# The inverse roots of the norms: a power on GpSimd and one Newton step instead of an integer guess and three

## The chip, the cores and the metric

The kernel runs on one core of a Trainium2 chip. A core has a matrix engine (TensorE, PE in the profile, with its weight loads as PEld), a vector engine (VectorE, DVE), an activation engine (ScalarE, ACT), a general engine (GpSimd, POOL) and a queue that issues the transfers (SyncE, SP). Each engine works through its own list of instructions in order; semaphores let one wait for another. The metric is the device time of one execution in microseconds (us); lower is better.

## The reference, cut to what matters

One layer of a hybrid decoder over 1024 prompt tokens and 8 x 8 sample tokens, all in fp32, width 1024. Every sub-layer begins and ends with an RMS norm, and the state-space group has one of its own:

```python
def rmsnorm(x, g):
    y = x * lax.rsqrt(jnp.mean(x * x, axis=-1, keepdims=True) + EPS)
    return y * g

h = rmsnorm(x, g_mix_pre) * (1 + scale_m) + shift_m
proj = h @ w_in                        # short convolution group, z, x/B/C, dt
...                                    # convolutions, SSD scan in chunks of 128
yg = (y_ssd * silu(z)).reshape(b, L, 4, 256)
y_ssd = rmsnorm(yg, 1.0) * ssm_norm_g  # over 256 channels of each of 4 groups
mix = concatenate([y_sc, y_ssd]) @ w_out
x = x + gate_m * rmsnorm(mix, g_mix_post)
h2 = rmsnorm(x, g_ffn_pre) * (1 + scale_f) + shift_f
f = (silu(h2 @ w_gate) * (h2 @ w_up)) @ w_down
x = x + gate_f * rmsnorm(f, g_ffn_post)
```

So each token needs an inverse root of a mean square five times over: four times over 1024 channels, and once for each of four groups over 256.

## The kernel before, in words

The tokens are the 1024 of the prompt and the 64 samples, in 9 tiles of up to 128. Matrix products are exact to fp32 by splitting each factor into a high and a low part (ACT makes the high part, DVE the low one) and by three products for each pair of tiles (L334 to L336, L514 to L516, L1078 to L1080). Large products of the channel sub-layer and of the convolution group use a scheme with seven products for eight.

The stages, by time in the profile:

- 0 to 70 us, the head. Rows of x are loaded; ACT squares and sums them (`sum_sq`, L357), `rsqrt_of` gives the inverse roots (`rstd_x`), DVE scales the rows (`scale_x`, L372), PE turns them (`turn_x`, L383). This is done for three sets of three tiles, `norm_x(0)` before the rest, the others in a list of steps written out by hand (`steps`), which queues each step behind the one before on PE, DVE, ACT and POOL. Beside it come the modulation vectors from `w_ada` (`quarter_products` L244, `quarter_out` L251 to L258), the split of the first weights (on POOL for L312, behind the casts of `wdt`, L465 and L466) and the modulation (`modulate_in`, L479 to L481).
- to about 600 us, projections and the SSD scan, with the group norm (`norm`): squares on ACT, sums across channels by products with ones (L920), `rsqrt_of` for 9 columns at once, a product that spreads the roots over the partitions (`spread`, L291), and the scaling on DVE (L939). It is called four times.
- to about 1000 us, the output projection. Its tail (`mix_tail`) turns tiles back into rows (L1239), squares them and multiplies by the gate row (L1240, L1241, in `residual_rows`), takes `rsqrt_of`, adds to the residual on DVE (L1256), sums squares again (L357), takes `rsqrt_of` again, scales on ACT (L1348), and turns the rows back (L1356, L1358). It is run for tiles 0 to 3, 4 to 5 and 6 to 8, beside products of other tiles.
- to the end, the channel sub-layer, whose last products (`down`, L1758) run with `out_tail`, which again calls `residual_rows` for tiles 0 to 3, 4 to 6 and 7 to 8. For the first two of these the scaling is on ACT (L1253) and the addition on POOL (L1254); for the last set both are one DVE instruction (L1256), and the result is stored (L1716).

So `rsqrt_of` is called 16 times: three times for the head, four times in the group norm, six times in the tails of the output projection and three times at the end. It works on a small tile `sm` of 128 partitions and 2, 3, 4 or 9 columns, from a pool of four buffers that also holds the sums `ss`, which POOL clears (L1232).

The order of the instructions on each engine is settled when the kernel is built. A scheduler takes them in the order of the program, subject to the orders written by hand, and puts one ahead of another where it expects it to be ready sooner, by its own estimates. In the profile, instructions of other work therefore stand between those of one call of `rsqrt_of`.

Of the kernel before, what the change touches and what calls it, by code (L numbers as in the profile page):

```python
# [11 lines left out]
I32 = mybir.dt.int32  # L12
AF = mybir.ActivationFunctionType
ALU = mybir.AluOpType
PSUM = bass.MemoryType.PSUM

P = 128
# [16 lines left out]
def hymba_step(ctx, tc, i, o):  # L34
    nc = tc.nc
    mult, add, sub, mn, mx = ALU.mult, ALU.add, ALU.subtract, ALU.min, ALU.max
# [26 lines left out]
    def nm(s):  # L63
        ids[0] += 1
        return f"{s}_{ids[0]}"
# [23 lines left out]
    def const(shape, name, dt=F32):  # L89
        return cp.tile(shape, dt, tag=name, name=name)  # L90
# [104 lines left out]
    cT = const([P, KT, 32], "cT")  # L195
    nc.vector.tensor_copy(cT.rearrange("p a b -> p (a b)"), cps[:, :256])

    modT = const([P, 6, 2, 4, 9], "modT")
    modv = [modT[:, v].rearrange("p h q r -> p (h q) r") for v in range(6)]
    def ada_steps(rd):  # L200
# [74 lines left out]
    def rsqrt_of(src, w):  # L275
        n = src.shape[1]
        t = smp.tile([P, 3, 12], F32, tag="sm", name=nm("sm"))
        v, r, u = (t[:, j, :n] for j in range(3))
        nc.vector.tensor_scalar(v, src, 1.0 / w, EPS, op0=mult, op1=add)
        nc.vector.tensor_scalar(r.bitcast(I32), v.bitcast(I32), 1, None, op0=ALU.logical_shift_right)  # L280
        nc.vector.tensor_scalar(r.bitcast(I32), r.bitcast(I32), -1.0, float(0x5F3759DF), op0=mult, op1=add)
        for _ in range(3):
            nc.vector.tensor_tensor(u, r, r, op=mult)
            nc.vector.scalar_tensor_tensor(u, u, -0.5, v, op0=mult, op1=mult)
            nc.vector.scalar_tensor_tensor(r, u, 1.5, r, op0=add, op1=mult)
        return r

    def spread(r, n):
# [75 lines left out]
    def rstd_x(c):  # L364
        rx[c] = rsqrt_of(ssx[:, 3 * c:3 * c + 3], D)
# [199 lines left out]
    r = 0  # L565
# [97 lines left out]
    for b in range(3):  # L663
        aps = pz()
        n = 512 if b < 2 else NS
# [247 lines left out]
    def norm(g, y, new_sq, new):  # L913
# [9 lines left out]
        for c, (c0, n) in enumerate(CH):  # L923
# [7 lines left out]
            sums(c)  # L931
            yield
        r = rsqrt_of(ps[:, 0:9], 2 * P)
        yield
        for c, (c0, n) in enumerate(CH):
# [293 lines left out]
    def residual_rows(at, ts, G, res, u, banks, done, parts=((0, 4), (4, 4)), pool=(), halves=(slice(0, D),),  # L1229
                      squares=None):  # L1230
        ss = smp.tile([P, 3, 12], F32, tag="sm", name=nm("ss"))
        nc.gpsimd.memset(ss, 0.0)  # L1232
        for j, (k0, nk) in enumerate(parts):
            for tt, t in enumerate(ts):
                tn = size(t)
                cols = slice(k0 * P, (k0 + nk) * P)
                ps = banks[j][tt]()[:tn, :nk * P]
                for k in range(nk):
                    nc.tensor.transpose(ps[:, k * P:(k + 1) * P], at(k0 + k, t), ident)  # L1239
                nc.scalar.activation((squares or u[tt])[:tn, cols], ps, AF.Square, accum_out=ss[:tn, j, tt:tt + 1])  # L1240
                nc.vector.tensor_tensor(u[tt][:tn, cols], ps, (G[0] if t < 8 else G[1])[:tn, cols], op=mult)  # L1241
            if j < len(parts) - 1:
                yield
        n = len(ts)
        for j in range(1, len(parts)):
            nc.vector.tensor_tensor(ss[:, 0, :n], ss[:, 0, :n], ss[:, j, :n], op=add)
        r = rsqrt_of(ss[:, 0, :n], D)
        for tt, t in enumerate(ts):
            tn = size(t)
            for cols in halves:  # L1250
                v, w = res[tt][:tn, cols], u[tt][:tn, cols]
                if tt in pool:
                    nc.scalar.activation(w, w, AF.Copy, scale=r[:tn, tt:tt + 1])  # L1253
                    nc.gpsimd.tensor_tensor(v, v, w, op=add)  # L1254
                else:
                    nc.vector.scalar_tensor_tensor(v, w, r[:tn, tt:tt + 1], v, op0=mult, op1=add)  # L1256
                done(t, tn, res[tt], cols)
        yield
# [19 lines left out]
    for k in range(KT):  # L1278
        v = [(fx, btp, h2p)[(k > 3) + (k > 5)].tile([P, T], F32R, tag="bt" if k in (4, 5) else "fm", name=nm("hb"))
             for _ in range(2)]  # L1280
# [449 lines left out]
    for k in range(0, 6, 2):  # L1730
        raw = ffp[9, 0].tile([P, 2, D], F32, tag="ff", name=nm("rwd"))
        nc.sync.dma_start(raw, w_down[(16 + k) * P:(18 + k) * P, :].rearrange("(k p) n -> p k n", p=P))
        for kk in range(2):
            v = wdp.tile([P, 2, D], F32R, tag="wd", name=nm("wd"))
# [12 lines left out]
    for ts in ([0, 1, 2, 3], [4, 5, 6], [7, 8]):  # L1747
        c0, n = ts[0] * P, sum(map(size, ts))
# [47 lines left out]
```

## Time and profile before

| | |
|---|---|
| median of 3 runs | 1732.71 us (1731.55 to 1736.04) |
| the profiled execution, its time | 1732.75 us |
| its span | 1731.0 us |
| PE busy | 1682.0 us, 97% of the span |
| PE weight loads | 1600.0 us, 92% |
| DVE busy | 1147.9 us, 66%, 2194 instructions |
| ACT busy | 770.9 us, 45% |
| POOL busy | 185.7 us, 11%, 277 instructions |
| mean granted clock of PE | 0.99 |

The span is the time from the first to the last instruction of the profiled execution; the rest of its time lies around it. A row of a timeline gives the start in us, the duration in us, the engine, the line, the operation, the output and inputs, the shapes and how often; in brackets stands the idle time of the engine before it and what ended it. In a list by tile or by line, durations are in ns (least, median, most). In a table of windows each engine has its busy time in that stretch, then come the granted PE clock, the share of the transfer engines that was busy, and GB/s. In the list of waits, the three numbers are the us in total, the times and the longest.

### The profile page before, as it was taken

The page shows a single profiled execution, that of the slowest core. Times are in us where ns is not written, and L with a number is a line of the kernel's source. Part 1 is how long each engine was busy: PE and PEld are TensorE (multiplying, and loading weights), DVE is VectorE, ACT ScalarE, POOL GpSimd, SP SyncE. Part 2 cuts the span into 40 slices and gives each one's busy share as a digit, 9 for nine tenths or more (in the row PEclk, how much of TensorE's full clock was granted, in tenths as well). Part 3 has the DMA queues.
Part 4 walks back from the last instruction along what each step waited for, and adds up shares of the span by engine and source line. Part 5 has one row for each costly group of instructions (what it writes and reads, how often), then busy time and mean ns, then how long its engine had stood idle before and what let it go on. Part 6 is the DMA issues. An engine that isn't in the chain of part 4 may idle for free. (4 is left out here: it accounts for less than half of the span.)

```text
span 1731.0 us, 31270 instructions
## 1 busy us (share of the span) xinstructions
PE 1682.0 (97%) x12604; PEld 1600.0 (92%) x12604; DVE 1147.9 (66%) x2194; ACT 770.9 (45%) x1571; POOL 185.7 (11%) x277
## 2 busy tenths in 40 slices
PE   5999999999999999999999999999999999999997
PEld 4898888899999999998989999999999999999987
DVE  5588677777798776661037779666666658588734
ACT  3457454657544433322226676444444446422222
POOL 2110001000001000000000000122222200122112
PEclk9999999999999999999999999999999999999999
DMA  9201344442322522348275643334433438865523
GB/s 321 73 21 30 113 152 151 148 131 77 109 69 77 177 70 74 113 165 301 69 255 183 195 134 140 121 140 142 147 131 140 148 123 312 314 230 198 203 92 134
DMA packets 159624, 256.37 MB, mean 148 GB/s; under 512 B 10578, under 2 KB 123394, under 8 KB 157943
## 3 DMA queue, kind: packets, MB, share of 16 engines
q1 hardware_dynamic: 159190, 253.19, 42.9%
q8 instruction: 99, 1.62, 0.4%
q10 hardware_dynamic: 288, 1.18, 0.2%
q14 instruction: 47, 0.38, 0.1%
HBM read 184.63 MB, written 69.71 MB: 147 GB/s over the span
## 5 line engine op out<-in xcount | busy, mean ns | idle before, releaser
L312 DVE TENSOR_TENSOR wl<-raw,wh 128x512 fp32r<-128x512 f32 (+1 forms) x87 | 61.3, 729 | 100.3 <-ACT wh L311 89.2
L334 PE MATMUL pm<-h,wh 128*128 128x384 f32 (+1 forms) x342 | 115.1, 337 | 0.1
L335 PE MATMUL pm<-h,wh 128*128 128x384 f32 (+1 forms) x342 | 114.9, 336 | 0.0
L336 PE MATMUL pm<-h,wl 128*128 128x384 f32 (+1 forms) x342 | 114.3, 335 | 0.0
L336 PE MATMUL pm<-hb,wl 128*128 128x512 f32 (+2 forms) x320 | 107.3, 337 | 2.1 <-DVE wl L312 2.1
L311 ACT CAST wh<-raw 128x512 fp32r<-128x512 f32 (+1 forms) x89 | 56.4, 665 | 116.2 <-PE pm L335 68.2
L335 PE MATMUL pm<-hb,wh 128*128 128x512 f32 (+2 forms) x320 | 107.4, 337 | 0.0
L334 PE MATMUL pm<-hb,wh 128*128 128x512 f32 (+2 forms) x320 | 105.8, 338 | 1.0 <-ACT wh L311 1.0
L1039 ACT CAST wd<-raw 128x256 fp32r<-128x256 f32 x112 | 42.9, 406 | 96.1 <-PE pz L1080 33.6
L1040 DVE TENSOR_TENSOR fs<-f,fs 128x576 fp32r<-128x576 f32 (+2 forms) x76 | 52.9, 710 | 25.3 <-ACT fs L1039 24.5
L336 PEld LDWEIGHTS pm<-hb,wl 128*128 128x128 f32 x320 | 60.8, 190 | 7.6 <-DVE wl L312 2.4
L334 PEld LDWEIGHTS pm<-h,wh 128*128 128x128 f32 x342 | 65.5, 191 | 1.9 <-issue 0.9
L335 PEld LDWEIGHTS pm<-h,wh 128*128 128x128 f32 x342 | 65.3, 191 | 1.4 <-issue 0.7
L334 PEld LDWEIGHTS pm<-hb,wh 128*128 128x128 f32 x320 | 60.3, 190 | 6.8 <-ACT wh L311 1.2
L336 PEld LDWEIGHTS pm<-h,wl 128*128 128x128 f32 x342 | 65.2, 191 | 1.3 <-issue 1.0
L1078 PE MATMUL pz<-fc,wd 128*128 128x288 f32 x224 | 66.2, 295 | 0.0
L1080 PE MATMUL pz<-fc,wd 128*128 128x288 f32 x224 | 66.0, 295 | 0.0
L1079 PE MATMUL pz<-fc,wd 128*128 128x288 f32 x224 | 65.9, 294 | 0.0
L335 PEld LDWEIGHTS pm<-hb,wh 128*128 128x128 f32 x320 | 60.8, 190 | 5.2
L1078 PE MATMUL pm<-fc,wd 128*128 128x256 f32 x224 | 63.3, 283 | 1.4 <-DVE facc L1095 1.4
L1040 DVE TENSOR_TENSOR wd<-raw,wd 128x256 fp32r<-128x256 f32 x112 | 54.4, 494 | 14.6 <-ACT wd L1039 14.2
L1080 PE MATMUL pm<-fc,wd 128*128 128x256 f32 x224 | 63.1, 282 | 0.3 <-DVE wd L1040 0.3
(5568 smaller groups left out, 6203.2 us busy)
## 6 DMA issues: line engine op xcount, KB each, us to landing
raw<-in_w_in SPq DMA_DIRECT2D x48, 512.0 KB
wa<-in_w_ada SPq DMA_DIRECT2D x32, 512.0 KB
raw<-in_w_out SPq DMA_DIRECT2D x32, 512.0 KB
f_d<-fs SPq DMA_DIRECT2D x28, 576.0 KB
f_d<-fs SPq DMA_DIRECT2D x30, 512.0 KB
raw<-in_w_gate SPq DMA_DIRECT2D x28, 512.0 KB
raw<-in_w_up SPq DMA_DIRECT2D x28, 512.0 KB
y_d<-y SPq DMA_DIRECT2D x26, 544.0 KB
```

Source lines behind the costliest of these rows:

```text
L311: (nc.gpsimd.tensor_copy if hi_eng else nc.scalar.copy)(wh, raw)
L312: (eng or nc.vector).tensor_tensor(wl, raw, wh, op=sub)
L334: mm(ps[:, :n], wh, xh, start=(first and j == 0), stop=False)
L335: mm(ps[:, :n], wh, xl, start=False, stop=False)
L336: mm(ps[:, :n], wl, xh, start=False, stop=(last and j == end))
L1039: nc.scalar.copy(hi, v)
L1040: (eng or nc.vector).tensor_tensor(lo, v, hi, op=sub)
L1078: mm(ps, W[0][k], X[0][k], start=(start and k == 0), stop=False, skip_group_check=True)
L1079: mm(ps, W[0][k], X[1][k], start=False, stop=False, skip_group_check=True)
L1080: mm(ps, W[1][k], X[0][k], start=False, stop=(stop and k == nk - 1), skip_group_check=True)
```

## The change

`rsqrt_of` computes v = mean square + eps on DVE as before. Before, the first guess at the root came from an integer shift and a subtraction from a constant (two DVE instructions), and three Newton steps of three DVE instructions each followed. Now POOL raises v to the power -0.5, with the exponents in a constant tile `half` of 128 x 12 that POOL fills once, and one Newton step of three DVE instructions follows. `rsqrt_of` is called in the same places with the same arguments.

```diff
     cT = const([P, KT, 32], "cT")
     nc.vector.tensor_copy(cT.rearrange("p a b -> p (a b)"), cps[:, :256])
 
+    half = const([P, 12], "half")
+    nc.gpsimd.memset(half, -0.5)
     modT = const([P, 6, 2, 4, 9], "modT")
...
         nc.vector.tensor_scalar(v, src, 1.0 / w, EPS, op0=mult, op1=add)
-        nc.vector.tensor_scalar(r.bitcast(I32), v.bitcast(I32), 1, None, op0=ALU.logical_shift_right)
-        nc.vector.tensor_scalar(r.bitcast(I32), r.bitcast(I32), -1.0, float(0x5F3759DF), op0=mult, op1=add)
-        for _ in range(3):
-            nc.vector.tensor_tensor(u, r, r, op=mult)
-            nc.vector.scalar_tensor_tensor(u, u, -0.5, v, op0=mult, op1=mult)
-            nc.vector.scalar_tensor_tensor(r, u, 1.5, r, op0=add, op1=mult)
+        nc.gpsimd.tensor_tensor(r, v, half[:, :n], op=ALU.pow)
+        nc.vector.tensor_tensor(u, r, r, op=mult)
+        nc.vector.scalar_tensor_tensor(u, u, -0.5, v, op0=mult, op1=mult)
+        nc.vector.scalar_tensor_tensor(r, u, 1.5, r, op0=add, op1=mult)
         return r
```

## The prediction

> **What bounds the kernel now.** I read the page first (busy time by engine), then the list of PE's waits, the table of windows, and last the timelines around each of the 16 calls of `rsqrt_of`.
>
> ```profile
> PE 1682.0 (97%) x12604; PEld 1600.0 (92%) x12604; DVE 1147.9 (66%) x2194; ACT 770.9 (45%) x1571; POOL 185.7 (11%) x277
> ```
>
> ```profile
> PE pm L336 <- DVE wl L312: 2.5, 2, 2.1
> PE pz L1356 <- ACT x L1348: 2.5, 2, 2.1
> ```
>
> ```profile
> 400.00:600.00 200.00, 197.46 (x1476) 190.56 (x1475) 167.75 (x321) 102.29 (x194) 5.84 (x14) 0.98 0.31 107
> 900.00:940.00 40.00, 37.87 (x242) 35.59 (x242) 27.63 (x56) 20.66 (x46) 0.13 (x1) 0.99 0.49 172
> 940.00:960.00 20.00, 20.00 (x154) 20.00 (x153) 12.37 (x30) 15.75 (x25) 0.00 (x0) 0.94 0.33 106
> 960.00:1000.00 40.00, 37.16 (x295) 36.31 (x294) 31.87 (x77) 26.84 (x57) 0.13 (x1) 0.96 0.77 243
> ```
>
> PE is busy for 97% of the span, so the change, which gives PE nothing less to do, can win only where PE waits, and at the end. Of the whole list of waits only two lie behind a call of `rsqrt_of` in the middle: 2.1 us for a weight part of L312 and 2.1 us for scaled rows of L1348. The windows place them (900 to 940, 960 to 1000) and show two more things: behind each of them PE's clock is granted at 0.94 and 0.96, and in the stage of the group norms (400 to 600) PE is busy for 197.46 of 200 us, although DVE is nearly full there (167.75 us). POOL, the last engine before the clock's column, is nearly idle in all four windows (5.84 of 200 us at most).
>
> **The change part by part.** First, what leaves DVE.
>
> ```profile
> L283 DVE TENSOR_TENSOR sm<-sm x48: 154/161/170, 11.7 to 1724.4; 128x3 f32<-128x3 f32 x18, 128x9 f32<-128x9 f32 x12, 128x4 f32<-128x4 f32 x9, 128x2 f32<-128x2 f32 x9
> ...
> L280 DVE TENSOR_SCALAR sm<-sm x16: 160/170/183, 11.3 to 1722.9; 128x3 int32<-128x3 int32 x6, 128x9 int32<-128x9 int32 x4, 128x4 int32<-128x4 int32 x3, 128x2 int32<-128x2 int32 x3
> ```
>
> Each of the 16 calls loses two integer instructions (170 ns) and six of the nine Newton instructions (161 ns): 16 x (2 x 0.170 + 6 x 0.161) = 20.9 us of DVE's busy time, hidden by PE except where DVE's lateness is PE's wait. What counts is the length of one call as a chain, and the last call shows it undisturbed:
>
> ```profile
> 1722.66 0.17 DVE L279 TENSOR_SCALAR sm<-ss 128x2 f32<-128x2 f32 x1
> ...
> 1724.83 0.16 DVE L285 SCALAR_TENSOR_TENSOR sm<-sm 128x2 f32<-128x2 f32 x1
> 1725.03 2.73 DVE L1256 SCALAR_TENSOR_TENSOR row<-row,sm,row 128x512 f32<-128x512 f32 x4
> ```
>
> Twelve instructions take 1725.03 - 1722.66 = 2.37 us, one each 0.197 us. After the change the chain is L279 (0.17), the hop to POOL, the power (call it p), the hop back, and three instructions (0.59). The hops are read from a place where POOL stands between two DVE instructions:
>
> ```profile
> 1076.96 0.68 DVE L1055 TENSOR_TENSOR raw<-raw,raw 128x512 f32<-128x512 f32 x1
> 1077.78 1.61 POOL L1057 TENSOR_TENSOR raw<-raw 128x512 f32<-128x512 f32 x1 [58.03 <-DVE raw L1055]
> 1079.43 0.69 DVE L1058 TENSOR_TENSOR raw<-raw,raw 128x512 f32<-128x512 f32 x1 [1.18 <-POOL raw L1057]
> ```
>
> L1055 ends at 1077.64 and POOL starts at 1077.78: 0.14 us. POOL ends at 1079.39 and L1058 starts at 1079.43: 0.04 us. The new chain is 0.17 + 0.14 + p + 0.04 + 0.59 = 0.94 + p, so a call wins 1.43 - p.
>
> No row shows a power, so p is bounded by POOL's other two-input instructions:
>
> ```profile
> L1368 POOL TENSOR_TENSOR acc<-acc,modT x8: 291/297/751, 1017.2 to 1019.5; 128x64 f32<-128x64 f32 x8
> L1254 POOL TENSOR_TENSOR row<-row,row x7: 2369/2397/2402, 1680.7 to 1713.4; 128x1024 f32<-128x1024 f32 x7
> ```
>
> An addition costs 297 ns for 64 columns and 2397 ns for 1024, 2.19 ns a column; carried down to 2 columns this is 0.297 - 62 x 0.00219 = 0.16 us, and a power is not cheaper than an addition. From above I take the dearest instruction that POOL has here, 2.4 us. Between the ends p stands nearest to the first row, of the same form and few columns; as a power is more work for each element than an addition, I take twice that row, 0.6 us. At that p a call wins 0.83 us.
>
> Now the places where a call is exposed.
>
> The last call (above) holds the last additions, which hold the stores; nothing else runs. It wins the full 0.83 us.
>
> The call for tiles 0 to 3 in the tail of the output projection:
>
> ```profile
> 927.89 0.17 DVE L279 TENSOR_SCALAR sm<-ss 128x4 f32<-128x4 f32 x1
> ...
> 931.50 4.88 DVE L1256 SCALAR_TENSOR_TENSOR x<-y,sm,x 128x1024 f32<-128x1024 f32 x4
> ...
> 937.06 1.28 DVE L312 TENSOR_TENSOR wl<-raw,wh 128x512 fp32r<-128x512 f32 x2
> 937.79 0.41 PE L336 MATMUL pm<-hb,wl 128*128 128x304 f32 x1 [2.13 <-DVE wl L312]
> ```
>
> PE waits 2.13 us for a weight part that stands on DVE behind four long additions, and these stand behind the call. Whatever the call loses, this wait loses, up to 2.13: 0.83 us if DVE stands still for the whole of the power, 1.43 if it fills that time with the work that stands between now. Which of the two, the head tells:
>
> ```profile
> 18.55 4.68 POOL L312 TENSOR_TENSOR wl<-raw,wh 128x1024 fp32r<-128x1024 f32 x2
> 21.43 1.84 DVE L258 SCALAR_TENSOR_TENSOR A_m<-modT,vE 128x18 f32<-128x18 f32 x1
> 25.68 1.02 POOL L481 TENSOR_TENSOR bt<-xn,bt 128x384 fp32r<-128x384 f32 x1 [2.46 <-issue]
> 25.73 1.00 DVE L279 TENSOR_SCALAR sm<-ssx 128x3 f32<-128x3 f32 x1 [0.17 <-ACT sq L357]
> ```
>
> ```profile
> L258 DVE SCALAR_TENSOR_TENSOR A_m<-modT,vE x4: 178/179/1839, 21.4 to 51.5; 128x18 f32<-128x18 f32 x4
> ```
>
> L258 otherwise takes 179 ns and L279 170 (its row above), yet here they took 1.84 and 1.00 us and ended (23.27, 26.73) just as POOL's instructions ended (23.23, 26.70). DVE's work from and to SBUF is held while POOL works, so I take 0.83. The Trainium skill says this too (Advanced Engine Details and Errata, VectorE Performance Modes): the second Vector port is shared with GpSimd, and the two block each other; by that rule the call wins 0.83 us, and if only DVE's dependent instruction waited it would win 1.43 and the sum below would be 0.6 us lower; the trace agrees with the rule by the two rows above.
>
> Two calls side by side, whose roots ACT waits for, and PE for ACT:
>
> ```profile
> 991.40 0.17 DVE L279 TENSOR_SCALAR sm<-ss 128x3 f32<-128x3 f32 x1
> ...
> 993.87 2.19 ACT L1348 ACTIVATE x<-x,sm 128x1024 f32<-128x1024 f32 x2 [3.04 <-DVE sm L285]
> 995.07 0.66 PE L1356 MATMUL pz<-ident,x 128*128 128x128 f32 x4 [2.11 <-ACT x L1348]
> ```
>
> They run woven into each other on DVE and take 2.4 us as one alone does. Afterwards two powers stand behind each other on POOL: 0.28 + 0.14 + 2p + 0.04 + 0.59 = 1.05 + 2p = 2.25 us, against 2.38. The pair wins 1.33 - 2p = 0.13 us.
>
> The second call of the head (L279 at 25.73) is followed by scaling, turning and this wait:
>
> ```profile
> 29.52 1.40 PE L383 MATMUL pz<-ident,y 128*128 128x128 f32 x6 [0.71 <-PE pm L516]
> ```
>
> It wins 0.83, of which PE can use 0.71; the head has other waits behind it, so I take half, 0.35 us.
>
> Costed at nothing are: the first call of the head, whose scaled rows lead to L258, and that is held until 23.27 by POOL in any case (ready at 21.43 + 0.2, so 1.6 us in hand; with that cover gone it would win 0.83); the third call of the head, the four of the group norms, the other three in the tails of the output projection and the first two of the last tail, all beside PE's own products (197.46 of 200 us in the window of the norms; were that cover gone, each would win up to 0.83). Clearing `half` is one more short instruction on an idle POOL. On DVE the instructions behind a waiting Newton step are the ones already held by the old chain. The power is put behind the clearing of `ss` (L1232) and, in the last tail, before the additions of L1254, which need its result.
>
> Sum: 0.83 + 0.83 + 0.13 + 0.35 = 2.14 us. The profiled execution took 1732.75 us, its span 1731.0; the median of the three is 1732.71, the same. Forecast: 1732.75 - 2.1 = 1730.6 us. With p from 0.16 to 1.2 it runs from 1728.5 (1.27 + 1.27 + 1.01 + 0.71 = 4.3 us won) to 1733.3. All of this is small: a difference of 0.3%, 5.2 us, is about what a measurement of this kernel can tell from none.
>
> **The rivals.**
>
> The power is long (ends on the other side). On each exposed place the loss is then whole: three calls at 1.43 - p and the pair at 1.33 - 2p give 5.62 - 5p. It turns into a loss from p = 1.12 us, and into more than 5.2 us from p = 2.16. At the upper bound, p = 2.4, the kernel takes 6.4 us more: 1739.1. For it speaks that no power is in the trace and each element may cost many steps; against it, that the tiles have 2 to 9 columns and POOL's short instructions cost 0.3 us.
>
> The power waits in POOL's queue. POOL is in order, and in the head it has transfers to wait for:
>
> ```profile
> 11.09 0.17 DVE L279 TENSOR_SCALAR sm<-ssx 128x3 f32<-128x3 f32 x1 [0.86 <-ACT sq L357]
> 13.46 2.47 DVE L372 TENSOR_SCALAR x<-x,sm 128x512 f32<-128x512 f32 x6
> 17.75 0.29 POOL L465 CAST wdt<-st 128x128 fp32r<-128x128 f32 x1 [13.68 <-DMA st<-in_w_in]
> 18.13 0.46 POOL L466 TENSOR_TENSOR wdt<-st,wdt 128x128 fp32r<-128x128 f32 x1
> ```
>
> If the first power is put behind these two, it starts at 18.6 and the rows are scaled from 18.59 + 0.6 + 0.04 + 0.59 = 19.8 instead of 13.46 (L372's start), 6.4 us later; less the 1.6 in hand this is 4.7, less the 2.1 won elsewhere 2.6: 1735.3 us. Against it: the sums of squares are complete at 11.1, and the transfer that L465 waits for comes only at 17.7. The Trainium skill has a rule that would do much the same (GPSIMD Engine Reference, Instruction dispatch): the first call of a freshly loaded kernel costs some 6 us more; by that page, an estimate, the total would be about 1735. L466, POOL's first addition of this kind, shows no such delay with 0.46 us; no row shows it for a power.
>
> The order shifts. Each engine's order is drawn up anew from estimates when the kernel is built, and the two waits of 2.1 us come from such an order. If both go, with the clock that is missing behind them (20 us at 0.94 and 40 at 0.96 are 1.2 and 1.6 us), the two places win 2.1 + 1.2 + 2.1 + 1.6 = 7.0, with 1.27 and 0.71 at end and head 9.0: 1723.7 us. The same shift can add such a wait with its clock, 3.3 us, which with the 2.1 won is 1733.9.
>
> Nothing moves: PE finds its waits elsewhere as soon as these shrink, and the time stays at 1732.7 us.
>
> **How the numbers follow.** Forecast (p up to 1.2 us) 0.55; nothing moves 0.10; long power 0.15; queue, first call or an added wait 0.13; both waits gone 0.07. Faster by over 0.3% (under 1727.5) are the last case and a little of the first: 0.10. Slower by over 0.3% (over 1737.9) are most of the long power and a little of the queue: 0.17. The rest, 0.73, lies within. The range for 8 in 10 leaves out the lowest and the highest cases: 1727.0 to 1739.0.
>
> **What would show it.** Right: a power of 0.3 to 1 us on POOL, starting 0.1 to 0.2 us behind L279 in all 16 calls; the last chain from L279 to L1256 at 1.5 us instead of 2.37; PE's wait for L312 near 938 at about 1.3 us; PE's busy time unchanged, DVE's lower by some 20 us. Wrong: powers of over 1.1 us; a power that starts more than 1 us behind L279 on a POOL that waits for a transfer; waits of PE at places where it had none.

## The result and the profile after

The changed kernel takes 1740.94 us (median), the kernel before took 1732.57 beside it: a ratio of 1.0051, 95% interval 1.0036 to 1.0067, some 8.8 us slower (microseconds won or lost are the ratio times the time before, here and below). The forecast was 1730.6. The profiled execution took 1742.65 us (span 1740.9). Two executions far outside, one of this kernel (2607 us at a granted clock of 0.587) and one of the fourth experiment (4180 us at 1.00), are left out of the ratios and are not explained here. The other executions of this kernel spread over some 16 us, before's over some 10, and where an execution is long its mean granted TensorE clock tends to be low (1733.5 us at 0.994, 1749.8 us at 0.987). Small differences are therefore read from the interval, and a profile is used to find the place.

In the changed kernel the lines are 2 higher up to the assignment of `v` (L281, before L279); the power is L282, the Newton step L283 to L285, and from L286 on the numbers are those of before. The page's line of busy times after the change:

```profile
PE 1682.4 (97%) x12604; PEld 1599.0 (92%) x12604; DVE 1132.4 (65%) x2066; ACT 769.0 (44%) x1569; POOL 205.8 (12%) x294
```

DVE gave up 15.5 us (1147.9 before; 20.9 were forecast, and two held instructions shown below take 4.3 of them back). PE's busy time is the same, so the time went into PE's idle time. The list of PE's waits after (total, times, longest), of which the first stood at 4.0 us before:

```profile
PE pz L383 <- DVE x L372: 15.1, 1, 15.1
...
PE pm L336 <- DVE wl L312: 4.1, 3, 3.5
...
PE pm L1078 <- ACT h L1039: 2.0, 1, 2.0
PE pz L1356 <- ACT x L1348: 1.8, 2, 1.4
PE pz L291 <- DVE sm L285: 1.5, 2, 0.9
```

One wait grew by 11 us, in the head, where the rows of x are scaled (L372) before PE turns them (L383). The timeline of POOL, then of DVE, at that place (start, duration, what, and the idle time before it with its releaser):

```profile
17.39 0.29 POOL L465 CAST wdt<-st 128x128 fp32r<-128x128 f32 x1 [13.26 <-DMA st<-in_w_in]
17.76 0.45 POOL L466 TENSOR_TENSOR wdt<-st,wdt 128x128 fp32r<-128x128 f32 x1
18.18 0.87 POOL L282 TENSOR_TENSOR sm<-sm,half 128x3 f32<-128x3 f32 x1
19.01 4.66 POOL L312 TENSOR_TENSOR wl<-raw,wh 128x1024 fp32r<-128x1024 f32 x2
```

```profile
11.05 0.17 DVE L281 TENSOR_SCALAR sm<-ssx 128x3 f32<-128x3 f32 x1 [1.43 <-ACT sq L357]
...
19.08 2.31 DVE L283 TENSOR_TENSOR sm<-sm 128x3 f32<-128x3 f32 x1 [7.85 <-POOL sm L282]
21.42 2.27 DVE L284 SCALAR_TENSOR_TENSOR sm<-sm 128x3 f32<-128x3 f32 x1
23.73 0.16 DVE L285 SCALAR_TENSOR_TENSOR sm<-sm 128x3 f32<-128x3 f32 x1
23.92 2.47 DVE L372 TENSOR_SCALAR x<-x,sm 128x512 f32<-128x512 f32 x6
```

Read the two side by side. `v` is ready at 11.22, but the power stands in POOL's queue behind L465 and L466, and L465 waits for a piece of `in_w_in` until 17.39. That is 7.0 us between `v` and the power, although the power itself takes 0.87. Then a second delay follows at once: POOL goes on with its two instructions of L312 (19.01 to 23.67), and two Newton instructions of DVE last 2.31 and 2.27 us, each until one of the two ends, where 0.16 is their usual length. L372 starts at 23.92 instead of 13.46, 10.5 us late. The chain of work that ended last now runs through exactly these pieces:

```profile
10.49 6.84 DMA st<-in_w_in
19.08 2.32 DVE sm L283
21.42 2.28 DVE sm L284
24.46 5.57 PE pz L383 x24
```

By the end of the head (the first product of L334 behind it, at 66.46 us before and 74.88 now) 8.4 us of the 10.5 are left, and most of it stays to the end of the kernel.

How long is a power? The costliest groups of POOL, kept apart by shape (busy time, mean ns of one):

```profile
L282 POOL TENSOR_TENSOR sm<-sm,half 128x9 f32<-128x9 f32 x4 | 8.5, 2121 | 55.9 <-DVE sm L281 55.9
...
L282 POOL TENSOR_TENSOR sm<-sm,half 128x3 f32<-128x3 f32 x6 | 5.1, 854 | 47.2 <-DVE sm L281 47.1
...
L282 POOL TENSOR_TENSOR sm<-sm,half 128x4 f32<-128x4 f32 x3 | 3.4, 1134 | 238.8 <-DVE sm L281 238.8
...
L282 POOL TENSOR_TENSOR sm<-sm,half 128x2 f32<-128x2 f32 x3 | 2.1, 700 | 48.9 <-DVE sm L281 48.9
```

It costs about 0.2 us for each column beyond two: 0.70 us for 2 columns, 2.12 for the 9 of the group norms. That is longer than the 1.43 us that the eight DVE instructions taken out give back once the two hops are paid.

The last call did what was forecast (DVE's timeline at the end; of the four instructions of L1256 the row shows the first two):

```profile
1733.37 0.17 DVE L281 TENSOR_SCALAR sm<-ss 128x2 f32<-128x2 f32 x1
1734.42 0.16 DVE L283 TENSOR_TENSOR sm<-sm 128x2 f32<-128x2 f32 x1 [0.88 <-POOL sm L282]
...
1735.01 1.41 DVE L1256 SCALAR_TENSOR_TENSOR row<-row,sm,row 128x512 f32<-128x512 f32 x2
```

From L281 to L1256 it is 1.64 us instead of 2.37, 0.73 won. The place at 940 did the opposite (DVE's timeline, then PE's):

```profile
938.84 0.17 DVE L281 TENSOR_SCALAR sm<-ss 128x4 f32<-128x4 f32 x1
940.13 0.17 DVE L283 TENSOR_TENSOR sm<-sm 128x4 f32<-128x4 f32 x1 [1.12 <-POOL sm L282]
...
940.73 4.87 DVE L1256 SCALAR_TENSOR_TENSOR x<-y,sm,x 128x1024 f32<-128x1024 f32 x4
...
945.90 1.28 DVE L312 TENSOR_TENSOR wl<-raw,wh 128x512 fp32r<-128x512 f32 x2
```

```profile
946.64 0.41 PE L336 MATMUL pm<-hb,wl 128*128 128x304 f32 x1 [3.49 <-DVE wl L312]
```

The call is shorter (1.89 us from L281 to L1256 instead of 3.61), yet PE waits 3.49 us for the weight part instead of 2.13. DVE's timeline inside the call before, and ahead of the call after, shows what changed:

```profile
929.24 0.69 DVE L312 TENSOR_TENSOR wl<-raw,wh 128x512 fp32r<-128x512 f32 x1
929.84 0.16 DVE L283 TENSOR_TENSOR sm<-sm 128x4 f32<-128x4 f32 x1
929.91 0.69 DVE L312 TENSOR_TENSOR wl<-raw,wh 128x512 fp32r<-128x512 f32 x1
```

```profile
935.05 1.29 DVE L312 TENSOR_TENSOR wl<-raw,wh 128x512 fp32r<-128x512 f32 x2
```

Before, two weight parts lay in the gaps of the call, and from the end of the second (930.60) to the next (937.06) were 6.5 us. Now DVE stands idle for 1.12 us during the power, the last parts ahead of the call end at 936.34, and the next come at 945.90: 9.6 us. PE waits 1.4 us longer for weights.

### The profile page after: what moved, and what is told of

It reads as the page before. It is cut to its first block, busy times and chain, and to the rows that moved or that the text cites. A ratio compares the mean times of both kernels' runs of the same rounds, so it can differ in the third digit from the quotient of the medians.

```text
span 1740.9 us, 31161 instructions
## 1 busy us (share of the span) xinstructions
PE 1682.4 (97%) x12604; PEld 1599.0 (92%) x12604; DVE 1132.4 (65%) x2066; ACT 769.0 (44%) x1569; POOL 205.8 (12%) x294
## 4 chain that ended last, share of the span: by engine, by line
PE 84%; DVE 8%; ACT 3%; DMA 2%; issue 2%; POOL 1%; SPq 0%; POOLq 0%; DVEq 0%; ACTq 0%
PE pm L334 10%; PE pm L336 10%; PE pm L335 10%; PE pz L1080 7%; PE pz L1078 7%; PE pz L1079 7%; PE pm L1080 7%; PE pm L1078 7%; PE pm L1079 7%; PE pm L211 1%; PE pz L751 1%; PE pz L745 1%; PE pz L756 1%; PE pz L723 1%; PE pz L291 1%
## 5 line engine op out<-in xcount | busy, mean ns | idle before, releaser
L312 DVE TENSOR_TENSOR wl<-raw,wh 128x512 fp32r<-128x512 f32 (+1 forms) x87 | 61.1, 729 | 97.3 <-ACT wh L311 83.4
L334 PE MATMUL pm<-h,wh 128*128 128x384 f32 (+1 forms) x342 | 114.8, 336 | 0.0
L334 PE MATMUL pm<-hb,wh 128*128 128x512 f32 (+2 forms) x320 | 105.7, 337 | 1.0 <-ACT wh L311 1.0
L1039 ACT CAST wd<-raw 128x256 fp32r<-128x256 f32 x112 | 42.9, 406 | 96.0 <-PE pz L1080 34.0
L1040 DVE TENSOR_TENSOR fs<-f,fs 128x576 fp32r<-128x576 f32 (+2 forms) x76 | 52.3, 701 | 25.8 <-ACT fs L1039 25.3
L334 PEld LDWEIGHTS pm<-h,wh 128*128 128x128 f32 x342 | 65.8, 192 | 1.5 <-issue 1.0
L334 PEld LDWEIGHTS pm<-hb,wh 128*128 128x128 f32 x320 | 60.4, 190 | 7.0 <-ACT wh L311 1.4
L282 POOL TENSOR_TENSOR sm<-sm,half 128x3 f32<-128x3 f32 (+3 forms) x16 | 19.1, 1194 | 390.8 <-DVE sm L281 390.7
L1078 PE MATMUL pm<-fc,wd 128*128 128x256 f32 x224 | 63.2, 282 | 1.0 <-DVE facc L1095 1.0
L1040 DVE TENSOR_TENSOR wd<-raw,wd 128x256 fp32r<-128x256 f32 x112 | 54.8, 497 | 13.9 <-ACT wd L1039 13.5
```

What stands on the lines that cost most here:

```text
L282: nc.gpsimd.tensor_tensor(r, v, half[:, :n], op=ALU.pow)
L312: (eng or nc.vector).tensor_tensor(wl, raw, wh, op=sub)
L334: mm(ps[:, :n], wh, xh, start=(first and j == 0), stop=False)
L1039: nc.scalar.copy(hi, v)
L1040: (eng or nc.vector).tensor_tensor(lo, v, hi, op=sub)
L1078: mm(ps, W[0][k], X[0][k], start=(start and k == 0), stop=False, skip_group_check=True)
```

## The experiments

Theory: most of the loss is POOL's queue in the head (the power behind two instructions that wait for a transfer); the rest comes from the later calls, because the power there is long or puts other work later. Rivals: the power is simply long everywhere; or the first Newton steps, held by POOL's L312, are the loss and not the wait for the transfer. Each kernel was timed beside the kernel before, which took 1731.06 us (first four), 1732.89 (next four) and 1731.25 (last two).

**1. The first power ahead of L465 and L466.**

```diff
+    first_pow = next(x for x in reversed(nc.cur_bb.bb.instructions) if x.engine == nc.gpsimd.engine)
...
+    with tc.issue_after(first_pow):
         nc.gpsimd.tensor_copy(wdt[:, :, 0:16], wdt_raw)
         nc.gpsimd.tensor_tensor(wdt[:, :, 16:32], wdt_raw, wdt[:, :, 0:16], op=sub)
```

> The changed kernel, with the two POOL instructions on wdt (cast and difference) queued behind the first power instead of ahead of it; nothing else is altered. Theory 'head' (the loss is the first power's place in POOL's queue, behind a transfer, and what follows from it): the first power starts near 11.2 us, scaling (L372) near 12.9 us instead of 23.9, and the total falls by 8 to 10 us to 1731-1733 us. Theory 'length' (the powers, 0.70 to 2.7 us each, cost more than the instructions they replace, in all 16 calls, and the head is covered by its transfers): the total stays at 1738-1741. Theory 'order' (the loss is new waits from the redrawn order of all engines): no set value, anything from 1730 to 1742, with waits of PE at other places.

Measured 1735.18 us, ratio 1.0027 (1.0014 to 1.0040). POOL's timeline and DVE's L372:

```profile
11.39 0.86 POOL L282 TENSOR_TENSOR sm<-sm,half 128x3 f32<-128x3 f32 x1 [7.26 <-DVE sm L281]
17.41 0.30 POOL L467 CAST wdt<-st 128x128 fp32r<-128x128 f32 x1 [5.16 <-DMA st<-in_w_in]
```

```profile
12.88 2.47 DVE L372 TENSOR_SCALAR x<-x,sm 128x512 f32<-128x512 f32 x6
```

With only these two instructions put behind it, the power starts 0.08 us behind `v` and L372 at 12.88, 0.6 us ahead of before. About half of the loss is gone, less than the 8 to 10 us that theory 'head' expected. That half of it stays, says that the later calls lose too. The 0.6 us also do not last to the end of the head, because there PE waits for weights that a transfer brings. ACT's cast of them in this kernel (in the kernel before it started at 60.81):

```profile
62.63 1.04 ACT L311 CAST wn<-raw 128x1024 fp32r<-128x1024 f32 x1 [7.32 <-DMA raw<-in_w_in]
```

That this is later than before is not the doing of the early call: in the fourth, fifth, sixth and ninth kernel, whose first call is the one of before, the cast starts at 61.23 to 61.92.

**2. The Newton steps freed of POOL's L312.** The power stays behind L465 and L466, and the two splits of weights on POOL are put behind a tiny copy of the first root.

```diff
+    seen = const([P, 3], "seen")
+    nc.gpsimd.tensor_copy(seen, rx[0])
+    seen_ins = next(x for x in reversed(nc.cur_bb.bb.instructions) if x.engine == nc.gpsimd.engine)
...
+    with tc.issue_after(seen_ins):
+        split_w(*w_first[0], raw_w[0], nc.gpsimd)
+        split_w(*w_first[1], raw_w[1], nc.gpsimd)
```

> The changed kernel, with the first power still behind the wdt instructions, but POOL's two long differences of the first weights (4.7 us together) put behind a small copy on POOL that reads the result of the first Newton step, so that DVE's Newton instructions do not meet them. Theory 'head', with its second half (DVE's Newton instructions are held by POOL's long differences): scaling starts near 18.2 + 0.87 + 0.04 + 0.59 = 19.7 us instead of 23.9, the total falls by some 4 us to about 1737. If the hold costs nothing (only the place in the queue does): 1741. 'Length': 1741.

Measured 1742.21 us, ratio 1.0058 (1.0041 to 1.0074): no gain in the total, where 4 us were expected. POOL's timeline, then DVE's:

```profile
19.51 5.01 POOL L312 TENSOR_TENSOR wl<-raw,wh 128x1024 fp32r<-128x1024 f32 x2
```

```profile
18.94 0.16 DVE L284 SCALAR_TENSOR_TENSOR sm<-sm 128x3 f32<-128x3 f32 x1
19.14 0.16 DVE L285 SCALAR_TENSOR_TENSOR sm<-sm 128x3 f32<-128x3 f32 x1
19.34 6.65 DVE L372 TENSOR_SCALAR x<-x,sm 128x512 f32<-128x512 f32 x6
```

The Newton steps are back at 0.16 us, but now the six scalings run beside L312 and take 6.65 us instead of 2.47: they end at 25.99, against 26.39 in the changed kernel. Whichever DVE instructions come beside POOL's two differences lose time there: 4.3 us in the Newton steps, 4.2 in the scalings. The rival that only the held Newton steps cost is not borne out. One thing stays unexplained: PE can begin to turn rows earlier here, and in this trace the first product of L334 comes at 70.30 instead of 74.88, 4.6 us that the total does not show.

**3. and 4. The power in the first call alone, and in all calls but the first.** The other calls keep the integer guess and three steps.

```diff
+        power = not rx          # the fourth kernel: power = bool(rx)
+        if power:
             nc.gpsimd.tensor_tensor(r, v, half[:, :n], op=ALU.pow)
+        else:
+            nc.vector.tensor_scalar(r.bitcast(I32), v.bitcast(I32), 1, None, op0=ALU.logical_shift_right)
+            nc.vector.tensor_scalar(r.bitcast(I32), r.bitcast(I32), -1.0, float(0x5F3759DF), op0=mult, op1=add)
+        for _ in range(1 if power else 3):
```

> Only the first of the 16 calls uses the power (placed as in the changed kernel, behind the wdt instructions); the other 15 use the integer guess and three steps. 'Head': the whole loss is here, 1740-1743 us. 'Length': 1733-1734 us. 'Order': between.

> The first call uses the integer guess and three steps, the other 15 the power and one step. 'Head': 1731-1733 us, the time before or a little less. 'Length': 1740 us. 'Order': between.

Measured 1738.70 us, ratio 1.0040 (1.0026 to 1.0055), for the first call alone, and 1735.34 us, 1.0019 (1.0008 to 1.0030), for all but the first. So the first call costs 6.9 us (0.40%) and the 15 others 3.3 us (0.19%); together 0.59%, within the interval of the whole change (0.51%, 0.36 to 0.67). Neither 'head' (the whole loss in the first call) nor 'length' holds alone.

**5. and 6. The 15 others taken apart: the power in the four group norms alone, and in the nine calls of the tails alone.**

```diff
-        power = not rx
+        power = w == 2 * P      # the sixth kernel: power = w == D and len(rx) == 3
```

> The power with one Newton step only in the four group norms (9 columns); the other 12 calls keep the integer guess and three steps. The power took 1.80 to 2.71 us there, more than the 1.43 us that the steps removed give back, and spread's wait for the root (L291, two waits, 1.5 us, longest 0.9) is new in the changed kernel. Theory A (the group norms carry what the 15 later calls cost, +3.3 us over before): the ratio is about 1.002, 1736 us against 1732.5, with the new wait L291 <- L285 in PE's list. Theory B (the output projection's tail carries it, through the wait for L312 of 3.5 instead of 2.1 us): the ratio is 1.000, within 0.001.

> The power with one Newton step only in the nine calls of the tails (2 to 4 columns), behind the norms; the head and the norms keep the integer guess and three steps. My prediction's terms there: 0.83 at the end, 0.83 at the wait for L312, 0.13 at the pair, 1.8 us won. Theory A (the norms carry the +3.3 us): ratio 0.999 to 1.000, 1731 to 1732.5. Theory B (DVE standing idle for the power near 940 puts the weight part of L312 later): PE's wait for L312 is 3 us or more, and the ratio is 1.001 to 1.002.

The norms alone: 1734.81 us, ratio 1.0016 (1.0002 to 1.0030). The tails alone: 1732.59 us, 0.9996 (0.9982 to 1.0011). By these ratios the norms carry the loss of the later calls and the tails come out about even (the interval would also hold the 1.8 us forecast), though the wait for L312 did grow as the second theory had it. PE's waits with the power in the tails alone, where L318 is L312 and L1362 is L1356 of before:

```profile
PE pm L342 <- DVE wl L318: 4.1, 3, 3.5
...
PE pz L1362 <- ACT x L1354: 1.8, 2, 1.4
```

The wait for L312 lost 1.4 us, the pair won 0.7 and the last call 0.7: the sum is nothing. The wait for L312 is 3.5 us in every kernel here with the power and its Newton step in the tails, and 2.1 to 2.3 in every one with the guess and three steps there. In the norms the changed kernel shows what a call costs. DVE's, POOL's and PE's timeline at the first norm:

```profile
416.50 0.17 DVE L281 TENSOR_SCALAR sm<-pz 128x9 f32<-128x9 f32 x1 [1.25 <-PE pz L920]
```

```profile
416.75 1.81 POOL L282 TENSOR_TENSOR sm<-sm,half 128x9 f32<-128x9 f32 x1 [38.74 <-DVE sm L281]
```

```profile
419.78 0.91 PE L291 MATMUL pz<-ident,sm 128*128 128x128 f32 x6 [0.66 <-DVE sm L285]
```

The root is ready 3.1 us behind L281, sooner than the 4.7 of before (408.46 to 413.13), and still PE waits for it, because `spread` (L291) now stands earlier in PE's order: 3.3 us behind L281, where before it stood 4.9 us behind with other products ahead of it. Two such waits, 0.66 and 0.87 us, make 1.5 of the 2.8 us by the ratio; the fifth kernel has the same two (0.67 and 0.87). PE's busy time in the stage shows a little more (the columns are those of the table of windows). Before, then the power in the norms alone:

```profile
400.00:590.00 190.00, 187.46 (x1396) 180.56 (x1395) 162.11 (x311) 100.05 (x190) 5.44 (x12) 0.98 0.31 107
```

```profile
400.00:590.00 190.00, 185.36 (x1385) 177.89 (x1384) 157.26 (x278) 94.67 (x183) 14.72 (x18) 0.98 0.31 107
```

PE stands idle for 4.64 us instead of 2.54, 2.1 us more at the same clock. Beside the 1.5 in `spread`, its other waits moved: about 2.3 us for the two parts of `h` (L1039 and L1040; the first stands in the list after) replace 2.0 for a weight part of the same two lines, and 0.3 for the scan's state (L765) is new. The remaining 0.7 us is within the noise. The head's second and third calls, the remainder of the 15, come to 0.19 - 0.16 + 0.04 = 0.07%, not distinguishable from nothing.

**7. The guess with two steps instead of three, no power.** A shorter call without a hop to another engine.

```diff
-        for _ in range(3):
+        for _ in range(2):
```

> No power anywhere: the integer guess on VectorE with two Newton steps instead of three in all 16 calls (leaves out the third Newton step, so that the roots are right to about 5e-6 only). The chain gets shorter by 3 x 0.197 = 0.59 us a call with no hop to another engine and no place in POOL's queue. If a shorter chain is worth what my prediction counted (last call, wait for L312, part of the pair and of the second head call), this wins 0.59 x 4 = 2.4 us at most: ratio 0.9986 to 0.9995. If nothing of it reaches PE but the last call: 0.6 us, ratio 0.9997, which can't be told from 1.

Measured 1727.09 us, ratio 0.9965 (0.9952 to 0.9978): 6.1 us faster than before, and the fastest kernel of this study. It wins more than the upper end expected. At 940 DVE goes on weaving other work into the call, and the wait for L312 shrinks (PE's waits, then DVE's timeline inside the call):

```profile
PE pm L342 <- DVE wl L318: 2.3, 3, 1.7
```

```profile
926.71 0.68 DVE L318 TENSOR_TENSOR wl<-raw,wh 128x512 fp32r<-128x512 f32 x1
927.31 0.16 DVE L289 TENSOR_TENSOR sm<-sm 128x4 f32<-128x4 f32 x1
```

Part of the gain in these traces is clock. The windows from 410 to 470 us (PE, PEld, DVE, ACT and POOL busy, then the granted clock) of before, after and this kernel, in this order:

```profile
410.00:470.00 60.00, 60.00 (x460) 55.48 (x459) 47.62 (x106) 36.18 (x67) 0.15 (x1) 0.97 0.28 99
```

```profile
410.00:470.00 60.00, 59.07 (x449) 52.58 (x448) 41.58 (x89) 35.50 (x72) 4.66 (x3) 0.91 0.23 77
```

```profile
410.00:470.00 60.00, 60.00 (x487) 55.25 (x486) 47.29 (x103) 37.17 (x70) 0.15 (x1) 1.00 0.31 103
```

A clock of 0.91 takes 60 x 0.09 = 5.4 us of the window, 0.97 takes 1.8, and 1.00 nothing. That is one execution of each, the same 60 us but not quite the same work, and executions differ in it. Over all executions the mean granted clock is 0.9915 for this kernel and 0.9899 for the one beside it, so some of the 6.1 us may be clock; how much was not tested.

**8. The power without a Newton step, the first power ahead.**

```diff
         nc.gpsimd.tensor_tensor(r, v, half[:, :n], op=ALU.pow)
-        nc.vector.tensor_tensor(u, r, r, op=mult)
-        nc.vector.scalar_tensor_tensor(u, u, -0.5, v, op0=mult, op1=mult)
-        nc.vector.scalar_tensor_tensor(r, u, 1.5, r, op0=add, op1=mult)
```

> As the kernel with the first power ahead of wdt's two instructions (1.0027), but without the Newton step behind the power: the chain is 0.35 us + p (1.05 to 1.2 for 2 to 4 columns, 2.2 to 3.0 for 9) instead of 2.37 us. If the length of the calls is what costs, it becomes equal to or faster than before: ratio 0.998 to 1.000, the pair and the wait for L312 0.6 us shorter each. If it is the hop itself (DVE idle, or held while POOL works) that puts other work later: it stays at 1.002 to 1.003.

Measured 1733.24 us, ratio 1.0004 (0.9990 to 1.0017). A call is now 0.35 us + p: half of before's in head and tails (1.05 to 1.5 us), and 2.47 us in the norms, 0.1 more than before's. The kernel is equal to before, as was expected if the length of the calls is what costs, while the seventh gains 6.1 us with calls of 1.78 us. PE's waits (L333 is L312; L288 is `spread`):

```profile
PE pm L333 <- DVE wl L309: 3.5, 3, 2.9
...
PE pz L288 <- POOL sm L282: 2.7, 2, 1.8
```

In the tail both count. The wait for L312 is 0.6 us shorter than in the first kernel (3.5), by the length of the Newton step left out, and the longest wait of the pair fell from 1.4 to 0.6. But it is still 2.9 us, against 1.7 in the seventh kernel with the longer call, so the hop to POOL costs there too. In the norms the power's own length is enough: PE waits up to 1.8 us for it.

**9. and 10. Two steps in the norms alone, and in all calls but the norms.**

```diff
-        for _ in range(3):
+        for _ in range(2 if w == 2 * P else 3):    # the tenth kernel: 3 if w == 2 * P else 2
```

> The integer guess everywhere; two Newton steps instead of three in the four group norms only (leaves out their third step), three in the other 12 calls. Two steps in all calls gave 0.9965. Theory A (in the stage of the norms a call lies on the path of VectorE, and its length counts whichever way: the power there cost 2.8 us, a shorter chain gains): ratio 0.997 to 0.9985, 1728 to 1730 us, the waits of PE between 470 and 575 gone or shorter. Theory B (the norms lie beside PE's products, as the prediction had it, and only the power with its hop costs): ratio 0.9995 to 1.0005.

> The complement: two Newton steps in the 12 calls of head and tails, three in the four norms (leaves out the third step in those 12). By the prediction's own terms, with 0.59 us won a call: last call 0.59, wait for L312 0.59, pair 0.59, second head call 0.35, 2.1 us in all: ratio 0.9988. Theory A (the norms carry most of the 6.1 us of the two steps): 0.9985 to 0.9995. Theory B: nearly all of the 6.1 us is here, 0.9965 to 0.9975.

Measured 1728.44 us, ratio 0.9988 (0.9978 to 0.9998), and 1728.17 us, 0.9985 (0.9974 to 0.9996). Each half gains, 2.1 and 2.6 us; the first lies between the ranges of its two theories. The second agrees in its total with the prediction's terms for 0.59 us a call (2.1 us), but not place by place: the last call won 0.58 us, the wait for L312 0.4, and the pair's longest wait 1.5. The first says that the norms aren't covered, and PE's busy time in their stage agrees (the ninth kernel):

```profile
400.00:590.00 190.00, 188.73 (x1414) 182.13 (x1413) 162.46 (x304) 99.17 (x191) 6.12 (x14) 0.98 0.32 110
```

PE is idle for 1.27 us there instead of 2.54: where it waited 2.0 us for a weight part (L1039 and L1040) it now waits 0.6. The sum, 4.7 us, is short of the 6.1 of the seventh kernel; the intervals overlap, and what the two do together was not tested.

## Why the prediction was wrong

**First call, costed at nothing: failed, and this is the main step.** The prediction named the mechanism as a rival (the power behind L465 and L466) and worked out L372 at 19.8. It set it aside because in the trace the sums are complete at 11.1 and L465's transfer comes at 17.7. That argument compares when the data arrive; an in-order queue is filled in the order drawn up at build, and the trace of before could not show where the power would stand in it. The order shown by the changed kernel is L465, L466, power. With the chance of 0.13, shared with two other cases, the rival was far too low, and its price too: 4.7 us on balance in the head, where the first call alone costs 6.9. L372 was not 6.4 but 10.5 us late, because the prediction's chain of 0.59 us for the Newton step did not count L312, which POOL starts right behind the power and which holds two of its steps for 4.3 us. The prediction had the two rows that show this (L258 and L279 held by POOL) and used them for another place. It also counted 1.6 us as in hand, of which 0.6 were there: the instruction it counted them at (L258, now L260) ended at 33.10 instead of 23.27, 9.8 us late. PE waited 15.1 us for L372 where it had waited 4.0. The long wait isn't a first-call load of code: the Trainium skill (GPSIMD Engine Reference, Instruction dispatch) puts that at some 6 us, and no such delay is in the first power, which took 0.87 us where the six powers of 3 columns take 0.854 on average.

**Length of the power, 0.6 us: too low.** 0.70, 0.85, 1.13 and 2.12 us for 2, 3, 4 and 9 columns. These means lie inside the bounds given (0.16 to 2.4), though one power of 9 columns took 2.71; the mistake was one value for all widths, when the widest calls are the ones in the stage where DVE is nearly full.

**Wait for L312, 0.83 won: wrong sign.** It lost 1.36 (3.49 against 2.13). The prediction asked whether DVE would stand still during the power and took that it would, which was right (1.12 us idle). But it then counted the call's length only. Before, the gaps of the call held two weight parts for PE; with the gaps gone, PE waited longer behind a shorter call.

**The pair, 0.13: low.** The longest wait fell from 2.11 to 1.4 us. **The last call, 0.83: right** in form, 0.73 measured, and 0.1 less because p was 0.70. **The tails in sum:** 1.8 won forecast; the measured ratio is 0.9996, and its interval (0.9982 to 1.0011) does not tell 1.8 from nothing, but the three places add up to nothing in the traces.

**The group norms, hidden beside PE's products: wrong.** 197.46 of 200 us busy says that PE has work there, not that the order keeps it ahead of the root. The 2.5 us that PE was idle in that window were not looked into either, and two steps instead of three halve them. PE waited 0.66 and 0.87 us for the root in `spread`, and the power there costs 0.16% (0.02 to 0.30) while a shorter chain gains 0.12% (0.02 to 0.22).

**The long power as a rival** (sign turns at 1.12 us) holds for the norms' powers but does not explain the first call, whose power is 0.87 us. **The shifted order as a rival** holds in part: `spread` stands closer to its root, and the weight parts left the call. That bears on the 3.3 us of the later calls, not on the 6.9 of the first.

What stays open: where the 4.6 us go that the second kernel had won at the end of the head, and how much of the differences beyond the named waits is the granted clock.

## What to carry to other kernels

Before moving a step to an idle in-order engine, read what will stand ahead of it and right behind it in that engine's queue, at every call: an engine that is idle because it waits for a transfer holds everything queued behind that wait. A hop in the middle of a short chain can also take away the gaps that the other engine filled, so shortening the chain where it stands (one step fewer, 6.1 us won, at less exact roots) can beat moving it (8.8 us lost). A high busy share of the bounding engine does not show that a call is covered; look at the waits that are left, and at the distance between the producer and the consumer in the order.

## What the runs showed of the hardware

- A power on POOL costs about 200 ns more for each column ((2.121 - 0.700) / 7), between 2 and 9 columns; an addition there costs 2.19 ns a column between 64 and 1024.
- DVE instructions beside POOL's two-input work are held much longer than the rows of before suggested: 0.16 us became 2.31 and 2.27, ending with POOL's instructions, and six scalings of 2.47 us became 6.65 beside 5.01 us of POOL. The Trainium skill (Advanced Engine Details and Errata, GPSIMD Details) tells that GpSimd shares a read and a write interface with VectorE and conflicts with VectorE instructions in a 2-port mode or with two inputs in SBUF. The runs here agree: the two held Newton steps have two inputs in SBUF. Which mode the scalings, with one such input, ran in is not shown.
- The granted clock fell below full speed in a stretch in which PE was busy throughout (0.97 between 410 and 470 in the kernel before, 60.00 of 60 us busy), so PE's waits in the same window can't be its only cause; how the clock is granted is not shown here.
